# Mean squares from the transposed input: the opening of a hybrid encoder step on one core

## The chip, the core and the metric

The kernel runs on one core of a Trainium2 chip. Five engines work side by side, each through its own instructions in order: TensorE (PE in the profile; its weight loads are PEld), VectorE (DVE), ScalarE (ACT), GpSimd (POOL) and SyncE (SP), which here only issues DMA transfers. The metric is the device time of one execution in microseconds (us), lower is better. The matrix products run in a reduced single-precision form (float32r): each operand is split into a high and a low part, and three products (high by high, high by low, low by high) stand for one.

## The reference, cut to what matters

One step of a one-layer encoder. Prompt frames (1024) and sample frames (8 streams of 16, so 128) are normalised, projected by one large matrix into eight groups of 1024 columns, go through two kinds of attention, are gated, and are projected back. What the change touches is the normalisation ahead of the first projection:

```python
def rms_norm(x, g):
    xf = x.astype(jnp.float32)
    y = xf * lax.rsqrt(jnp.mean(xf * xf, axis=-1, keepdims=True) + EPS)
    return (y * g.astype(jnp.float32)).astype(x.dtype)
...
    h = rms_norm(xp, norm_pre[l])
    q_sb, k_sb, v_sb, gate_sb, q_r, k_r, v_r, gate_r = project(h, w_in[l], pos_p)
```

The width of a frame (D_MODEL) is 2048, so each frame has one mean square over 2048 elements.

## The kernel before, in words

The frames are taken in two groups. Group 0 holds prompt tiles 0 to 3 and the sample tile, 640 frames, in two pieces of 256 and 384 frames (`X_PIECES`); group 1 holds the other four prompt tiles, 512 frames. For projection the input must lie transposed: 128 of the 2048 features on the partitions, frames along the free axis. Sixteen blocks (`KT`) of 128 features make the whole. The host hands over the transposed input as `x_cols`; the input by rows (`x_rows`) is there as well.

The opening (the `p0` pools, lines 489 to 563) does this for group 0, one piece after the other:

- `load_x` (L503) brings row tiles of 128 frames by 2048 (1 MB each, two buffers of tag `xt`), and `mean_square` (L514) squares each in one ScalarE instruction that also sums along the row. The first piece has two row tiles, the second three.
- `inv_rms` (L173 to L179) makes the inverse root of the mean: VectorE scales and adds, ScalarE takes the root, VectorE takes the reciprocal and corrects it in four steps. The operand has one column a row tile.
- `spread` turns that column into a row, the same on all partitions: VectorE puts it on a diagonal (`dg`, L522), TensorE multiplies by a matrix of ones in full single precision (L524, two records a product in the trace), and ScalarE copies the result (`rb`, L525).
- `load_cols` (L510) brings the transposed input of the piece in four chunks of four blocks (`xc`, four buffers). `normal` multiplies a block by the gain and by `rb`: odd blocks by ScalarE (gain, L530) and GpSimd (`rb`, L531), even ones by VectorE in one instruction (L533). `split` (L164, L165) makes the high part by ScalarE and the low part by VectorE.
- `products` (L378) multiplies the blocks by the panels of two weight columns, 4 and 5 (the retention queries and keys of head 0): twelve instructions a panel and quarter, so 96 a piece. Panels are loaded in four parts (`wr`, 256 KB each, five buffers shared by all weight loads; L367 and L548) and split like the input. Both panels' parts are kept, because both pieces need them.

Behind the opening follow the rotary step of both results (`rope`, L468 to L472), the retention values (`ret_values`, rows of weights as moving operand, L434) and the gate. Beside these a job, `stage_rest`, prepares group 1 in the same manner: it loads four row tiles, squares them, spreads the result, scales sixteen blocks and stores them to `s_h` by ScalarE's queue (L587). A job is a generator; every product calls `tick`, which lets a due job take one step, and the number that a job yields is the count of ticks until its next step. Group 1 itself is loaded from `s_h` much later (L248, buffers `mr`).

The order of the instructions on each engine isn't written out: a planner goes through the program by order of writing and by its own costs, and puts an instruction ahead of others written earlier when these aren't ready by its reckoning. `pin` keeps an instruction, in that planning alone, behind the last product written so far. Each engine then works strictly in the planned order. The accumulators lie in four PSUM banks (`acc0`, `acc1`, two each), which both panels' results hold until the rotary step has read them; `pb` has four banks of its own.

Of the kernel before, what the change touches and what calls it, by code (L numbers as in the profile page):

```python
# [11 lines left out]
F32 = mybir.dt.float32  # L12
F32R = mybir.dt.float32r
AF = mybir.ActivationFunctionType
ALU = mybir.AluOpType
# [73 lines left out]
def tile_hybrid_step(  # L89
# [358 lines left out]
    with ExitStack() as s1:  # L448
# [42 lines left out]
        with tc.tile_pool(name="p0", bufs=2) as p0, tc.tile_pool(name="p0s", bufs=1) as p0s, tc.tile_pool(  # L491
# [9 lines left out]
            def load_x(t):  # L501
                xt = p0.tile([P, D], F32, name="xt", tag="xt", bufs=2)
                nc.sync.dma_start(xt, x_rows(t))  # L503
                return xt

            def load_cols(piece, k, m):
                o, n = X_PIECES[piece]
                xc = p0.tile([P, m, n], F32, name=f"xc{piece}", tag="xc", bufs=4)
# [4 lines left out]
            def mean_square(xt, ssq, i):  # L513
                nc.scalar.activation(xt, xt, AF.Square, accum_out=ssq[:, i : i + 1])  # L514

            def spread(ssq, n, hold=None):
                rstd = inv_rms(p0, ssq[:, :n], D, f"p0{n}")
# [10 lines left out]
            def normal(dst, xc, k, rb, pool):  # L528
                if pool:
                    nc.scalar.activation(xc, xc, AF.Copy, scale=pre[:, k : k + 1])  # L530
                    nc.gpsimd.tensor_tensor(dst, xc, rb, ALU.mult)  # L531
                else:
                    nc.vector.scalar_tensor_tensor(dst, xc, pre[:, k : k + 1], rb, ALU.mult, ALU.mult)  # L533

            tiles = g0["tiles"]
            accs = [acc_banks(g0), acc_banks(g0)]
            at = 0
            weights4 = []
            for piece, n in enumerate((2, 3)):
                o, m = X_PIECES[piece]  # L540
                ssq = p0s.tile([P, n], F32, name=f"ssq{n}")
                xts = [load_x(t) for t in tiles[at : at + n]]
                xcs = [load_cols(piece, w * WQ, WQ) for w in range(KT // WQ)]
                if piece == 0:
                    weights4 = [list(load_w(col(4, 0))), []]
                    for w in range(KT // WQ):
                        wr = wp.tile([P, WQ, P], F32, name="wr", tag="wr", bufs=5)
                        nc.sync.dma_start(wr, w_cols[COLS.index(5), 0, :, w * WQ : (w + 1) * WQ, :])  # L548
                        wh, wl = (p0s.tile([P, WQ, P], F32R, name=f"w{s}5{w}") for s in "hl")
                        split(wh, wl, wr)  # L550
                        weights4[1].append((w, wh, wl))
                for i, xt in enumerate(xts):
                    mean_square(xt, ssq, i)
# [992 lines left out]
```

## Time and profile before

| | |
|---|---|
| median of 3 runs | 2297.87 us (2295.14 to 2300.01) |
| the profiled execution | 2302.97 us, span 2301.2 us |
| TensorE busy | 2242.1 us, 97% of the span |
| VectorE, ScalarE, GpSimd busy | 54%, 40%, 16% |
| TensorE's first weight product | 17.61 us after the span's start |
| moved by DMA | 470.99 MB, mean 205 GB/s |

The profiled execution is 5.1 us above the median, and 1.8 us of it lie around the span. Rows of the trace in order of time give the start, the duration (of several merged instructions together), the engine, the line, the operation, the tiles written and read, shapes and count; in brackets stands how long the engine was idle before it and what it waited for. Rows of groups give busy time, mean duration in ns, idle time before, and its causes. Rows of stages give from and to, the length, busy time and count for each engine (TensorE, weight load, VectorE, ScalarE, GpSimd), the clock granted to TensorE as a share of full speed, the DMA engines' share and GB/s; where the rows are those of one line alone, only the engines that this line uses stand in them. A queue that issues DMA transfers has a q behind its engine (SPq).

### The profile page before, as it was taken

The numbers are of one execution on the slowest core, as the hardware profiler recorded it, in microseconds if no ns is written. First come the engines' busy times: TensorE is split into PE (matmuls) and PEld (weight loads), VectorE is DVE, ScalarE is ACT, GpSimd is POOL, SyncE is SP. The second block draws the span as 40 slices with busy tenths as digits, with TensorE's granted clock in tenths as the row PEclk, the third lists the DMA queues.
The fourth block names the chain that finished last, engine by engine and source line by source line (L and its number), as shares of the span: only waits on it lengthen the run. The fifth ranks groups of instructions, "written<-read, shape, count | busy, mean of one in ns | idle before, by whom it ended". The sixth has DMA issues, their size and how long they took to land.

```text
span 2301.2 us, 38949 instructions
## 1 busy us (share of the span) xinstructions
PE 2242.1 (97%) x14306; PEld 2021.9 (88%) x14306; DVE 1236.9 (54%) x2534; ACT 919.4 (40%) x1960; POOL 357.5 (16%) x593
## 2 busy tenths in 40 slices
PE   5999999999999999999999999999999999999998
PEld 4999999999999999999887989898888987788886
DVE  6534444354534435356556565656565566556577
ACT  6423333333333333334433433343343444535363
POOL 2012030120203021121102111120212212000020
PEclk9999999999999999999999999999999999999999
DMA  7856657565566658568778788778787767766596
GB/s 282 280 186 195 190 151 223 175 191 195 148 194 199 197 159 229 169 185 266 198 214 224 218 213 236 211 231 223 220 220 224 211 167 186 238 215 185 142 224 175
DMA packets 441552, 470.99 MB, mean 205 GB/s; under 512 B 182416, under 2 KB 302224, under 8 KB 439696
## 3 DMA queue, kind: packets, MB, share of 16 engines
q1 hardware_dynamic: 318112, 304.09, 46.3%
q0 software_dynamic: 28720, 78.41, 12.1%
q10 hardware_dynamic: 94528, 86.00, 11.8%
q8 instruction: 112, 1.84, 0.3%
q14 instruction: 80, 0.66, 0.1%
HBM read 363.51 MB, written 114.29 MB: 208 GB/s over the span
## 4 chain that ended last, share of the span: by engine, by line
PE 87%; DMA 6%; DVE 3%; issue 2%; ACT 2%; POOL 0%; SPq 0%; DVEq 0%; ACTq 0%; POOLq 0%
PE acc L378 46%; PE accn L434 16%; PE a L1179 5%; PE a L1180 5%; PE a L1176 5%; PE pa L762 2%; PE z L732 2%; PE zc L801 1%; PE pd L865 1%; DMA s_be<-be 1%; DMA ro<-s_rk 1%; DMA be<-s_be 1%; PE pa L910 1%; DMA s_rk<-rk 1%; DMA xt<-x_prompt 1%
## 5 line engine op out<-in xcount | busy, mean ns | idle before, releaser
L378 PE MATMUL acc<-mh,wh 128*128 128x256 f32 (+2 forms) x2304 | 668.0, 341 | 7.2 <-ACT wh L164 4.4
L378 PE MATMUL acc<-ml,wh 128*128 128x256 f32 (+2 forms) x2304 | 664.3, 340 | 1.2 <-DVE ml L165 1.1
L378 PE MATMUL acc<-mh,wl 128*128 128x256 f32 (+2 forms) x2304 | 661.0, 339 | 1.3 <-DVE wl L165 1.3
L165 DVE TENSOR_TENSOR wl<-wr,wh 128x512 fp32r<-128x512 f32 x504 | 346.0, 689 | 468.0 <-ACT wh L164 450.2
L164 ACT ACTIVATE wh<-wr 128x512 fp32r<-128x512 f32 x504 | 316.9, 631 | 651.1 <-PE acc L378 331.6
L378 PEld LDWEIGHTS acc<-mh,wh 128*128 128x128 f32 x2304 | 421.8, 189 | 40.0 <-ACT wh L164 4.9
L378 PEld LDWEIGHTS acc<-ml,wh 128*128 128x128 f32 x2304 | 423.3, 189 | 34.2 <-issue 3.3
L378 PEld LDWEIGHTS acc<-mh,wl 128*128 128x128 f32 x2304 | 426.0, 189 | 29.8 <-DVE wl L165 2.0
L434 PE MATMUL accn<-whn,mh 128*128 128x256 f32 x1152 | 328.8, 285 | 1.3 <-DVE rq L471 0.9
L434 PE MATMUL accn<-wln,mh 128*128 128x256 f32 x1152 | 325.9, 283 | 0.0
L434 PE MATMUL accn<-whn,ml 128*128 128x256 f32 x1152 | 325.5, 283 | 0.0
L434 PEld LDWEIGHTS accn<-whn,mh 128*128 128x128 f32 x1152 | 220.8, 192 | 4.5 <-ACT whn L164 1.7
L434 PEld LDWEIGHTS accn<-wln,mh 128*128 128x128 f32 x1152 | 220.8, 192 | 0.8
L434 PEld LDWEIGHTS accn<-whn,ml 128*128 128x128 f32 x1152 | 220.5, 192 | 0.0
L165 DVE TENSOR_TENSOR wln<-wrn,whn 128x512 fp32r<-128x512 f32 x128 | 87.7, 687 | 140.6 <-ACT whn L164 139.2
L164 ACT ACTIVATE whn<-wrn 128x512 fp32r<-128x512 f32 x128 | 80.6, 633 | 190.0 <-PE accn L434 92.9
L625 POOL DMA_DIRECT2D be<-s_be x128 | 94.1, 741 | 155.6 <-DMA s_be<-be 132.8
L661 DVE TENSOR_TENSOR_SCAN kp<-kp 128x1152 f32<-128x1152 f32 (+4 forms) x40 | 82.7, 2067 | 53.5 <-POOL kp L650 36.9
L650 POOL TENSOR_SCALAR_AFFINE_SELECT kb<-kb 128x128 f32<-128x128 f32 x64 | 30.5, 484 | 439.1 <-ACT kb L644 436.8
L788 POOL DMA_DIRECT2D kcT<-cache_k x64 | 34.6, 545 | 404.4 <-PE pd L865 268.9
L1179 PE MATMUL a<-wl,mh 128*128 128x512 f32 x240 | 93.6, 390 | 0.2 <-DVE wl L165 0.2
L1180 PE MATMUL a<-wh,ml 128*128 128x512 f32 x240 | 93.6, 390 | 0.0
(272 smaller groups left out, 2950.5 us busy)
## 6 DMA issues: line engine op xcount, KB each, us to landing
wr<-w_cols SPq DMA_DIRECT2D x384, 256.0 KB, 4.5
wrn<-w_rows SPq DMA_DIRECT2D x128, 256.0 KB, 3.8
kcT<-cache_k POOLq DMA_DIRECT2D x64, 512.0 KB, 8.3
vc<-cache_v SPq DMA_DIRECT2D x64, 512.0 KB, 5.8
wr<-s_b SPq DMA_DIRECT2D x80, 256.0 KB, 4.0
br<-w_out SPq DMA_DIRECT2D x64, 256.0 KB, 5.1
s_b<-br ACTq DMA_DIRECT2D x32, 512.0 KB, 5.4
wr<-w_out SPq DMA_DIRECT2D x48, 256.0 KB, 4.0
```

What stands on the lines that cost most here:

```text
L164: nc.scalar.activation(hi, src, AF.Copy),
L165: nc.vector.tensor_tensor(lo, src, hi.bitcast(F32), ALU.subtract),
L378: last = nc.tensor.matmul(a[:, :m], lhs[:, j, :], rhs[w][:, j, o : o + m], start=(w == 0 and j == 0 and n == 0), stop=(w == KT // WQ - 1 a ...
L434: anchor[0] = nc.tensor.matmul(a, lhs[q][:, jj, ts], rhs[:, j, :], start=(w == 0 and j == 0 and n == 0 and t % 2 == 0), stop=(w == KT // 2 ...
L625: q.dma_start(raw[32 * i : 32 * i + 32, :].rearrange("p (k a) -> p k a", a=32), s[:, :, 32 * i : 32 * i + 32].rearrange("k (j b) a -> b (k ...
L661: nc.vector.tensor_tensor_scan(rev, rev, rev, 1.0, ALU.mult, ALU.bypass)
L732: nc.tensor.matmul(z[:, :c], q2[a][:, i * P : (i + 1) * P], k2[b][:, s : s + c], start=(m == 0), stop=(m == 2),)
L762: nc.tensor.matmul(po[:, :P], at[:, j, :], vn[:, j, :], start=(j == 0), stop=(j == t))
L788: ready.append((kc, nc.gpsimd.dma_start(kc, cache_k[h, m // 4, m % 4])))
L1176: ins = nc.tensor.matmul(a, hi[k][:, ts], wh, start=first, stop=False)
L1179: nc.tensor.matmul(a, hi[k][:, ts], wl, start=False, stop=False)
L1180: anchor[0] = nc.tensor.matmul(a, lo[k][:, ts], wh, start=False, stop=last)
```

## The change

The mean squares of group 0 no longer come from row tiles. ScalarE squares the transposed blocks, and TensorE multiplies each by the matrix of ones and adds the sixteen results up in a PSUM bank; so the sums stand on all partitions at once, and `spread` is not called for group 0. `inv_rms` now works on the whole 128x256 or 128x384 operand. For the second piece GpSimd adds the squares of two neighbouring blocks first, so that eight products do. These squares are written in between the first piece's products: two chunks' worth after the second quarter, two after the third, pinned behind the products. The scaling (`normal`) is VectorE's alone. The order of the loads is written anew: transposed chunks of the first piece, then the parts of both panels, with second-piece chunks between; first-piece and second-piece chunks have four buffers each. The high parts of the second panel lie in the `mr` buffers. In `stage_rest` the row tiles are loaded and squared in halves of 1024 columns, with longer yields (10 for 6 after a load), and two partial sums are added.

```diff
             def load_x(t):
-                xt = p0.tile([P, D], F32, name="xt", tag="xt", bufs=2)
-                nc.sync.dma_start(xt, x_rows(t))
-                return xt
+                halves = []
+                for c in range(2):
+                    xt = p0.tile([P, HALF], F32, name="xt", tag="xc0", bufs=4)
+                    nc.sync.dma_start(xt, x_rows(t)[:, c * HALF : (c + 1) * HALF])
+                    halves.append(xt)
+                return halves
...
             def mean_square(xt, ssq, i):
-                nc.scalar.activation(xt, xt, AF.Square, accum_out=ssq[:, i : i + 1])
+                for c, half in enumerate(xt):
+                    pin(nc.scalar.activation(half, half, AF.Square, accum_out=ssq[:, c, i : i + 1]))
...
-            def normal(dst, xc, k, rb, pool):
-                if pool:
-                    nc.scalar.activation(xc, xc, AF.Copy, scale=pre[:, k : k + 1])
-                    nc.gpsimd.tensor_tensor(dst, xc, rb, ALU.mult)
-                else:
-                    nc.vector.scalar_tensor_tensor(dst, xc, pre[:, k : k + 1], rb, ALU.mult, ALU.mult)
+            def normal(dst, xc, k, rb):
+                nc.vector.scalar_tensor_tensor(dst, xc, pre[:, k : k + 1], rb, ALU.mult, ALU.mult)
...
+            totals = [p0p.tile([P, 512], F32, name=f"tot{i}", tag="pb")[:, :n] for i, (_, n) in enumerate(X_PIECES[:2])]
+            xcs = [[load_cols(0, w * WQ, WQ) for w in range(KT // WQ)], []]
+
+            def squares(piece, w):
+                sq = None
+                for j in range(WQ):
+                    k = w * WQ + j
+                    one = p0.tile([P, X_PIECES[piece][1]], F32, name=f"sq{piece}", tag=f"sq{j % 2}")
+                    pin(nc.scalar.activation(one, xcs[piece][w][:, j, :], AF.Square))
+                    if piece and j % 2 == 0:
+                        sq = one
+                        continue
+                    if piece:
+                        nc.gpsimd.tensor_tensor(one, one, sq, ALU.add)
+                    nc.tensor.matmul(totals[piece], ones, one, start=(k <= piece), stop=(k == KT - 1))
+
+            for w in range(KT // WQ):
+                squares(0, w)
...
+            first_panel = load_w(col(4, 0))
+            both_panels = [], []
+            for w in range(KT // WQ):
+                both_panels[0].append(next(first_panel))
+                both_panels[1].append(load_second(w))
+                if w:
+                    xcs[1].append(load_cols(1, (w - 1) * WQ, WQ))
+            xcs[1].append(load_cols(1, KT - WQ, WQ))
+            for piece, (o, m) in enumerate(X_PIECES[:2]):
+                rb = inv_rms(p0s, totals[piece], D, f"p0{piece}")
                 for w in range(KT // WQ):
                     for j in range(WQ):
                         k = w * WQ + j
-                        xn = p0.tile([P, m], F32, name=f"xn{piece}", tag="xn", bufs=3)
-                        normal(xn, xcs[w][:, j, :], k, rb, k % 2)
+                        xn = p0.tile([P, m], F32, name=f"xn{piece}", tag="xn", bufs=2)
+                        normal(xn, xcs[piece][w][:, j, :], k, rb)
                         split(mov[0][w][:, j, o : o + m], mov[1][w][:, j, o : o + m], xn)
-                    for acc, ws in zip(accs, weights4):
+                    for acc, ws in zip(accs, both_panels):
                         last = products(mov, acc[piece : piece + 1], g0["pieces"][piece : piece + 1], *ws[w])
-                at += n
+                    if piece == 0:
+                        for c in ((), (0, 1), (2, 3), ())[w]:
+                            squares(1, c)
```

More of the change, by code (lines that the diff above doesn't have):

```diff
@@ L539, in tile_hybrid_step @@
[L539 to L553, printed above, removed]
-                rb = spread(ssq, n)
+            def normal(dst, xc, k, rb):
+                nc.vector.scalar_tensor_tensor(dst, xc, pre[:, k : k + 1], rb, ALU.mult, ALU.mult)
```

23 lines of the change are left out of this document (14 added, 9 removed).

## The prediction

> **What bounds the kernel now.** I read the page first, then TensorE in order of time over the first 100 us, then the other engines there, and last the groups by form for prices.
>
> ```profile
> PE 2242.1 (97%) x14306; PEld 2021.9 (88%) x14306; DVE 1236.9 (54%) x2534; ACT 919.4 (40%) x1960; POOL 357.5 (16%) x593
> ```
>
> TensorE is busy for 97% of the span, so only time in which it stands still or runs at half clock can be won. The change touches nothing but the opening and the staging behind it. There TensorE goes like this (start, duration):
>
> ```profile
> 17.61 0.58 PE L378 MATMUL acc<-mh,wh 128*128 128x256 f32 x1 [3.56 <-ACT wh L164]
> ...
> 22.87 0.41 PE L378 MATMUL acc<-mh,wh 128*128 128x256 f32 x1
> 23.08 0.41 PE L378 MATMUL acc<-ml,wh 128*128 128x256 f32 x1
> ...
> 23.87 0.28 PE L378 MATMUL acc<-mh,wh 128*128 128x256 f32 x1
> 23.98 0.28 PE L378 MATMUL acc<-ml,wh 128*128 128x256 f32 x1
> ...
> 34.43 0.28 PE L378 MATMUL acc<-mh,wl 128*128 128x256 f32 x1
> 40.09 1.97 PE L524 MATMUL pb<-dg,ones 128*128 128x128 f32 x6 [5.38 <-DVE dg L522]
> 44.06 1.01 PE L378 MATMUL acc<-mh,wh 128*128 128x384 f32 x2 [2.00 <-ACT mh L164]
> ...
> 45.53 0.52 PE L378 MATMUL acc<-mh,wl 128*128 128x384 f32 x1
> 45.85 0.52 PE L378 MATMUL acc<-mh,wh 128*128 128x384 f32 x1
> ...
> 64.86 0.29 PE L434 MATMUL accn<-whn,mh 128*128 128x256 f32 x1
> ...
> 67.55 0.36 PE L434 MATMUL accn<-whn,mh 128*128 128x256 f32 x1 [0.85 <-DVE rq L471]
> ...
> 71.72 0.35 PE L434 MATMUL accn<-whn,mh 128*128 128x256 f32 x1 [0.46 <-DVE rk L471]
> ```
>
> The first piece's 96 products run from 17.61 to 34.7. A gap of 9.4 us follows, broken by three small products. The second piece's 96 run from 44.06 to 64.86. Spacing tells the clock: 0.21 us for 256 columns until 23.08, 0.11 to 0.12 from 23.87 on; 0.32 us for 384 columns at 45.53. The granted clock fell in the gap and came back 7.2 us after TensorE took up work at 40.09:
>
> ```profile
> 37.00:38.00 1.00, 0.00 (x0) 0.00 (x0) 0.00 (x0) 1.00 (x2) 0.00 (x0) 0.56 0.98 393
> ...
> 46.00:47.00 1.00, 1.00 (x5) 1.00 (x4) 1.00 (x2) 0.63 (x2) 0.45 (x2) 0.50 1.20 225
> 47.00:48.00 1.00, 1.00 (x7) 1.00 (x6) 1.00 (x2) 0.84 (x2) 1.00 (x1) 0.82 0.64 197
> ...
> 55.00:60.00 5.00, 4.89 (x29) 4.58 (x28) 1.00 0.01 2
> ```
>
> The last row counts the products of L378 alone: 5.0 / 29 = 0.172 us each at full clock. Why the gaps are there stands on the other engines:
>
> ```profile
> 1.26 0.90 SPq L503 DMA_DIRECT2D xt<-x_prompt  x2
> ...
> 6.37 1.91 ACT L514 ACTIVATE xt<-xt 128x2048 f32<-128x2048 f32 x1 [4.06 <-DMA xt<-x_prompt]
> ...
> 8.89 1.91 ACT L514 ACTIVATE xt<-xt 128x2048 f32<-128x2048 f32 x1 [0.52 <-DMA xt<-x_prompt]
> ...
> 10.93 0.17 DVE L173 TENSOR_SCALAR p02v<-ssq 128x2 f32<-128x2 f32 x1 [9.28 <-ACT xt L514]
> ...
> 12.21 0.16 DVE L179 TENSOR_TENSOR p02r<-p02r,p02u 128x2 f32<-128x2 f32 x1
> ...
> 14.09 0.38 ACT L525 ACTIVATE rb<-pb 128x256 f32<-128x256 f32 x1 [0.70 <-PE pb L524]
> ...
> 28.59 0.33 SPq L503 DMA_DIRECT2D xt<-x_sample  x1
> ...
> 36.14 1.91 ACT L514 ACTIVATE xt<-xt 128x2048 f32<-128x2048 f32 x1 [3.09 <-DMA xt<-x_sample]
> ```
>
> Each row tile of 1 MB takes 2.52 us of transfer (6.37 to 8.89). The last one is issued at 28.59, when a buffer comes free, and lands at 36.1. Squares, root, spreading and rb follow; so the second piece waits for rows that exist only for their squares.
>
> **The change, part by part.** Times are those of the profiled execution; differences go onto the median of 2297.87.
>
> *Loads.* Five row tiles leave SP's queue, 12.6 us of transfer. The first xc chunk (half a tile's bytes) takes the first row tile's place and lands at 6.37 less half of 2.52, 5.1; the fourth at 8.9. The panels follow, with second-piece chunks between them. SP still waits for free wr buffers (five), now with second-piece chunks queued behind it.
>
> *First sums.* ScalarE squares a 128x256 block in 0.41 (cast row below), so TensorE starts at 5.5, into two of the pb banks. Nothing in the trace shows a sum of 256 columns; nearest is L524, in the same full-precision form with 128:
>
> ```profile
> 84.67 0.71 PE L524 MATMUL pb<-dg,ones 128*128 128x128 f32 x4
> 85.14 0.36 PE L434 MATMUL accn<-whn,ml 128*128 128x256 f32 x1
> ...
> L164 ACT ACTIVATE mh<-xn 128x256 fp32r<-128x256 f32 x16 | 5.8, 405 | 2.2 <-POOL xn L531 2.2
> L164 ACT ACTIVATE mh<-xn 128x384 fp32r<-128x384 f32 x16 | 7.9, 520 | 7.1 <-POOL xn L531 6.5 <-DVE xn L533 0.5
> L295 DVE TENSOR_TENSOR br<-br 128x256 f32<-128x256 f32 x192 | 80.3, 418 | 7.5 <-DMA br<-s_y 5.6
> L470 DVE TENSOR_TENSOR sw<-sw,sinT 128x384 f32<-128x384 f32 x16 | 8.9, 558 | 15.4 <-ACT sw L469 15.4
> L175 DVE RECIPROCAL or<-or 128x5 f32<-128x5 f32 x8 | 1.5, 189 | 8.1 <-ACT or L174 8.1
> L175 DVE RECIPROCAL or<-or 128x1 f32<-128x1 f32 x8 | 1.3, 158 | 1.0 <-ACT or L174 1.0
> L179 DVE TENSOR_TENSOR or<-or,ou 128x5 f32<-128x5 f32 x8 | 1.3, 166 | 0.3
> L179 DVE TENSOR_TENSOR or<-or,ou 128x1 f32<-128x1 f32 x8 | 1.3, 158 | 0.2
> ```
>
> The four records are two products; they took 0.47 at full clock (84.67 to 85.14), so one of 256 columns takes 0.24 (if width were free) to 0.47 (if time goes with columns). Columns rule elsewhere (0.11 at 256, 0.172 at 384), so I take 0.43, and 0.86 at half clock. In the opening the half clock lasted from 17.61 to past 23.08; I take 5.5 us: six and a half sums in that, nine and a half in 4.1. Totals stand at 5.5 + 5.5 + 4.1 + 0.2 = 15.3. Ends: 14.2 if the clock comes after the 3.3 us that passed between 44.06, when work became continuous, and the 0.82 slice; 19.5 if never. The Trainium skill, "TensorE: Matmul & The Clock Gate", Part 1, says that about 3.4 us of sustained work in a free-running window release the clock; by it the totals would stand at 14.3, one microsecond earlier, and this trace's 5.5 and 7.2 us (both with pauses) are longer.
>
> *Root chain, now 128x256.* Seven steps took 10.93 to 12.37 = 1.44 us at two columns. Widening adds 0.25 to each of four tensor steps (0.418 against 0.16), 0.21 to the root (0.405 against 0.19), 0.2 to a scalar step: 1.4. The reciprocal is unknown: +0.26 if it goes as TENSOR_TENSOR, +1.8 if its narrow slope (31 ns over four elements, 7.8 each) holds to 256. TENSOR_TENSOR's own narrow slope (8 ns, 2.0 each) is twice its wide one ((558 - 418) / 128 = 1.09), so I halve: +1.0. Spreading (dg, pb, rb) goes. The factors stand at 15.3 + 0.1 + 1.44 + 1.4 + 1.0 = 19.2, against 14.47 (14.09 + 0.38) before: 4.8 later. Ends 18.5 and 20.0.
>
> *First piece's products.* Block 0 needs a scaling, a cast and the semaphores: first product at 20.3 (17.61 before). VectorE now scales all sixteen blocks:
>
> ```profile
> 22.52 0.47 DVE L533 SCALAR_TENSOR_TENSOR xn<-xc,pre,rb 128x256 f32<-128x256 f32 x1
> ...
> 30.32 1.09 DVE L165 TENSOR_TENSOR ml<-xn,mh 128x256 fp32r<-128x256 f32 x3
> ...
> 47.20 1.38 DVE L165 TENSOR_TENSOR ml<-xn,mh 128x384 fp32r<-128x384 f32 x1
> ...
> L531 POOL TENSOR_TENSOR xn<-xc,rb 128x384 f32<-128x384 f32 x8 | 10.3, 1282 | 17.8 <-ACT rb L525 10.7 <-DVE ml L165 6.0 <-POOL xn L531 1.1
> ```
>
> Back to back that is 0.41 + 0.36 = 0.77 a block, 12.3 in all. Beside a GpSimd operation VectorE's 0.56 became 1.38, so each of the eight pair additions holds it up by 0.8: 6.6. Sum 18.9, until 38.1. TensorE needs 96 x 0.117 = 11.2, 2.5 more for 26 products at half clock (5.5 / 0.21, each 0.095 longer; it stood still from 15.3 to 20.3), and eight sums of 384 columns at 0.64 = 5.1: until 39.1. So the first piece ends at 39.1, not 34.7. ScalarE's sixteen squares of 0.52 stand in one queue with the casts; 14 us of its work fit beside 19. The panels' splits go into VectorE's wait before 19.2 and cost nothing while that wait lasts.
>
> *Second factors.* The additions of GpSimd (10.3 us) can start when the first half of the products is issued, about 26.6, so totals stand at 37.8. The chain at 384 columns: 1.44 + 4 x 0.39 + 0.33 + 0.25 + reciprocal 1.5 (0.4 to 2.9) = 5.1, and 0.3 of scaling beside it. Factors at 43.2, first product 1.2 later at 44.4, against 44.06: the gap that the rows made is filled by a later first piece and a wider chain.
>
> *Second piece.* TensorE has stood still for 5.3 us and starts at half clock: 17 products at 0.32, 79 at 0.172, together 19.0 (20.8 before, when GpSimd's scaling held VectorE up). VectorE needs sixteen times 1.05. End 63.4 against 64.86: 1.4 earlier.
>
> *Behind it.* The stalls at 67.55 and 71.72, 1.3 us, are acc banks whose rope copies stood behind 1.91 us squares on ScalarE. Halved and pinned squares take about 0.8 of that. The additional read-outs, VectorE's one addition, the longer yields and the later s_h stores cost nothing while ScalarE, VectorE and SP have slack there, and the mr buffers lent to the second panel are free by then; SP's mr loads wait for those stores, and if they came much later, panel loads behind them would be late. No GpSimd transfer lies in this stretch to be moved past.
>
> Sum: -1.4 - 0.8 = -2.2, from 2297.87 to 2295.7, inside the 0.2% (4.6 us) that a measurement of this kernel can tell from no change.
>
> **The rivals.**
>
> *The gaps close (faster).* Full clock fell by 37.4 (the 0.56 row), 2.7 us after 34.7. If the reciprocal costs like TENSOR_TENSOR, 0.7 and 1.1 us go, and if the second totals are ready some 2 us before the products end, the wait for the second factors is short enough to keep the clock: 2.5 more, and the overlap itself 1. Together 5.3 below the forecast: 2290.4. For it: GpSimd's additions are off the path; against it: its start hangs on ScalarE's queue.
>
> *Reciprocal at its narrow slope (no change).* 0.8 and 1.4 us more: 2297.9. The rows at one and five elements speak for it; no wide one is shown. The Trainium skill, "VectorE: DVE Perf Modes", "First, the fixed hardware budget", says that the reciprocal is an iterative divide with a repeat count of 8; read as eight cycles an element at its 0.96 GHz, an estimate, that is 2.1 and 3.2 us, and the time would be the same 2297.9. No run here shows it yet.
>
> *ScalarE's queue (slower).* Squares wait for sum buffers that GpSimd and TensorE give back, and casts behind them wait along. If the eight squares of a quarter pair stand ahead of its casts, the additions (5.1 us for four) run before the quarter's scaling and not beside it: per quarter 5.1 + 0.9 + 3.1 + 1.0 = 10.1 for 6.3, twice +3.8, and a TensorE without products: +7.6, 2303.3. It decides when six or more squares stand ahead. For it: ScalarE stood idle 6.5 us for GpSimd's results with casts behind (384 cast row above). Against it: a planner that sees the wait puts casts between.
>
> **How the numbers follow.** Forecast 0.32, slow reciprocal 0.12, gaps closed 0.32, ScalarE's queue 0.24. The first two are within 0.2%: 0.44; faster 0.32, slower 0.24. Term ends from the forecast: clock -1.0 to +4.2, reciprocal -1.8 to +2.2, hold-up by GpSimd 0 to -3 (half of the 6.6 where VectorE waits anyway), stalls -0.5 to +0.8. The forecast's own range is 2292 to 2299; over the cases it reaches from 2287 (gaps closed, and the clock early) to 2305 (the queue, and the clock late).
>
> **What would show it.** First sums at 5.5, their last near 15; a 256-wide reciprocal near 1.2 us; first product near 20, last of the first piece near 39; TensorE idle 5 us ahead of 44; last product of the second piece near 63; no waits of 0.8 for rope afterwards. The prediction is wrong if sums stay at 0.86, if casts wait more than 2 us behind squares, if the panels' splits on VectorE delay the first chain, or if a panel load stands behind a stalled SP queue.

## The result

The changed kernel takes 2315.98 us (median of 4 runs, 2311.55 to 2318.23), the kernel before 2297.36 beside it: a ratio of 1.0078, 95% interval 1.006 to 1.0097, so 18.6 us slower. A second set on another chip gave 1.0073 (1.0058 to 1.0088). The prediction was 2295.7, no change, with a range of 2287 to 2305: the sign of the change was missed.

The profiled execution of the changed kernel has a span of 2314.0 us (2301.2 before). Its engine totals:

```profile
PE 2258.5 (98%) x14344; PEld 2035.3 (88%) x14344; DVE 1245.4 (54%) x2546; ACT 918.4 (40%) x1972; POOL 348.6 (15%) x585
```

TensorE in order of time (start, duration), the changed kernel:

```profile
5.50 9.88 PE L551 MATMUL tot<-sq,ones 128*128 128x256 f32 x32 [5.50 <-ACT sq L545]
25.06 0.80 PE L378 MATMUL acc<-mh,wh 128*128 128x256 f32 x2 [9.68 <-ACT mh L164]
...
46.98 0.28 PE L378 MATMUL acc<-mh,wl 128*128 128x256 f32 x1
...
54.42 0.69 PE L378 MATMUL acc<-mh,wh 128*128 128x384 f32 x1 [7.16 <-ACT mh L164]
...
74.30 0.34 PE L378 MATMUL acc<-mh,wl 128*128 128x384 f32 x1
...
76.46 0.36 PE L434 MATMUL accn<-whn,mh 128*128 128x256 f32 x1 [0.29 <-DVE rq L471]
...
149.24 0.79 PE L931 MATMUL pa<-rv,sc 128*128 128x128 f32 x2 [6.14 <-DVE sc L915]
```

Two separate losses show. The opening (up to the second piece's last product) ends at 74.6 instead of 65. And at 149 there is a wait of 6.1 us that the kernel before doesn't have, far behind the code that changed. Stages of the changed kernel (from and to, length, busy time of TensorE, weight load, VectorE, ScalarE, GpSimd, granted clock, DMA share, GB/s):

```profile
40.00:60.00 20.00, 12.24 (x55) 9.79 (x54) 14.98 (x26) 9.10 (x20) 4.12 (x4) 0.83 0.14 43
...
140.00:160.00 20.00, 13.86 (x87) 13.67 (x86) 5.79 (x15) 3.98 (x12) 0.00 (x0) 0.83 0.51 154
```

In 40 to 60 the DMA engines move 43 GB/s (194 before, where two of group 1's row tiles are issued at 45.39 and 46.34; in the changed kernel such a load goes out last at 41.18), and no compute engine waits for a transfer there: the 7.16 us ahead of 54.42 are a wait for ScalarE's cast, which waits for VectorE's chain. In 140 to 160 TensorE stands still for 6.1 us (busy for all 20 us before). Until about 154.5 it then runs at half pace, two products in 0.53 us instead of 0.30, so the stall costs more than its length.

### The profile page after: what moved, and what is told of

Its sections match the earlier page's. It is cut to its first block, busy times and chain, and to the rows that moved or that the text cites. A ratio compares the mean times of both kernels' runs of the same rounds, so it can differ in the third digit from the quotient of the medians.

```text
span 2314.0 us, 39042 instructions
## 1 busy us (share of the span) xinstructions
PE 2258.5 (98%) x14344; PEld 2035.3 (88%) x14344; DVE 1245.4 (54%) x2546; ACT 918.4 (40%) x1972; POOL 348.6 (15%) x585
## 4 chain that ended last, share of the span: by engine, by line
PE 86%; DMA 6%; DVE 3%; issue 2%; ACT 2%; SPq 1%; POOL 1%; ACTq 0%; DVEq 0%; POOLq 0%
PE acc L378 46%; PE accn L434 16%; PE a L1200 5%; PE a L1201 5%; PE a L1197 5%; PE pa L783 2%; PE z L753 2%; PE zc L822 1%; PE pd L886 1%; DMA s_be<-be 1%; DMA wr<-w_cols 1%; DMA ro<-s_rk 1%; DMA be<-s_be 1%; PE pa L931 1%; PE pS L946 1%
## 5 line engine op out<-in xcount | busy, mean ns | idle before, releaser
L1197 PE MATMUL a<-wh,mh 128*128 128x512 f32 x240 | 93.4, 390 | 0.8 <-ACT wh L164 0.8
```

The source lines that it names most:

```text
L1197: ins = nc.tensor.matmul(a, hi[k][:, ts], wh, start=first, stop=False)
```

## The second loss: a collision of transfers

The staging is the job `stage_rest` that prepares group 1. Early runs changed its yields alone.

**e1**: the changed kernel with yields of 6.

```diff
-                    yield 10
+                    yield 6
```

> The changed kernel with the waits of stage_rest back at 6 ticks after a load (10 in the changed kernel). Theory A, two separate losses: the opening (first product of the retention values at 74.5 us, 64.9 before) and a later stall of 6.1 us at the first retention block of head 0, which comes because group 1's staging ends 17 us later (last s_h store issued at 124.4, 107.3 before), so that the cache loads of GpSimd's queue start at 130.8 (114.5 before) and run beside the turned keys' loads. By A the last store is issued near 115, the cache loads start before 122, the stall falls below 2 us, and the time is about 2308 (7 to 8 below the changed kernel's 2316). Rival B, the stall follows from the opening's lateness alone: stores move by less than 3 us, the stall stays near 6 us, time within 2 us of 2316.

Measured 2312.98, 1.0062 (1.0043 to 1.008). The wait shrank to 3.7 us only, and the last store came at 121.3: 3 us earlier, where theory A asked for 9. This run lies between A and B and decides little.

**e2**: the kernel before with yields of 10 (the same edit the other way).

> The kernel before with only the waits of stage_rest raised from 6 to 10 ticks after a load. Theory A: the last s_h store moves from 107.3 to about 116, the cache loads from 114.5 to about 122, and a stall at the first retention block comes up: 2300 to 2305 (before: 2297). Rival B, the waits matter only behind a late opening: within 2 us of 2297.

Measured 2303.68, 1.0023 (1.0014 to 1.0033), 6.6 us above the kernel before on its chip: longer yields alone cost time, and a wait of 4.5 us appears at the same products.

**e7**: the changed kernel with yields of 2.

> The changed kernel, with the staging's yields after loads at 2 instead of 10. Theory A (the end of the staging is a loss of its own: memory freed late, GpSimd's cache loads beside the transposing transfers): the last store to s_h comes at 102 to 107 (124.4 with 10, 121.3 with 6), the cache loads start near 110 (130.8), the 6.1 us stall at the sample scores is under 1.5, the first z product comes near 157 (163.2), and the time is 6 to 7 us lower, near 2309.5. Rival B (the stall comes from the later opening itself, whatever the staging does): the stall stays above 4 us and the time above 2313.

Measured 2309.52, 1.005 (1.0034 to 1.0066). The wait is gone, and the first z product (L753, the next attention scores) came at 157.6, as theory A has it, though the last store came at 116.9, 10 us later than it asked. So the time of the stores alone is not what decides. What decides is which of two kinds of transfer goes out first, and by how much. The rows, the changed kernel first: VectorE's first write into the memory that the opening gives back, GpSimd's loads of cached keys, SP's transposing loads, and the instruction that needs these, with its wait.

```profile
130.21 0.06 DVE L660 MEMSET kp<- 128x1 f32 x1 [3.46 <-DMA s_h<-xc]
...
130.82 3.39 POOL L809 DMA_DIRECT2D kcT<-cache_k  x6 [85.24 <-DMA wrn<-w_rows]
...
131.60 4.75 SPq L646 DMA_DIRECT2D ro<-s_rk  x4
...
146.77 0.84 DVE L1032 STREAM_TRANSPOSE rkn<-ro 128x640 f32<-128x640 f32 x1 [9.13 <-DMA ro<-s_rk]
```

The kernel before:

```profile
114.47 3.40 POOL L788 DMA_DIRECT2D kcT<-cache_k  x6 [54.41 <-DMA wr<-w_cols]
...
120.48 6.06 SPq L625 DMA_DIRECT2D ro<-s_rk  x4
...
131.50 0.84 DVE L1011 STREAM_TRANSPOSE rkn<-ro 128x640 f32<-128x640 f32 x1 [0.86 <-DMA ro<-s_rk]
```

The cache loads (six of 512 KB, issued within 3.4 us) go out when the opening's memory is free, and the last staged chunk must be stored for that: without the hold below, they start 5.4 to 8.6 us behind the issue of the last store in every run. VectorE's `kp` names that store as what it waited for; for GpSimd's first load the profile names a weight load. The transposing loads stand in SP's queue behind weight loads, which wait for buffers that VectorE's splits give back. In the changed kernel VectorE itself stands for the last store first (the row of `kp`), and SP's queue with it, so that both kinds of transfer follow the same store. Before, the cache loads had a lead of 6.0 us over the transposing ones; now 0.8, and `ro<-s_rk` takes 13.4 us to land (median of its four) instead of 9.8. VectorE's transposition waits 9.1 us, the scores behind it make TensorE wait 6.1. Over the runs the lead sorts the waits without exception: with 5.1 us or more (e7 5.1, e9 5.9, the kernel before 6.0, e14 6.1, e13 6.4, e12b 10.1, e16 12.7) there is no such wait; with 2.8 (e2) and 3.0 (e1) it is 4.5 and 3.7 us; with 0.8 or less (the changed kernel, e3, e4, e5b, e6, e10, e14c, e17) it is 5.2 to 7.2 us.

**e14c**: is it the staging or the late opening? The kernel before with VectorE's scaling (e9, below) and the changed staging, but with rows for the mean squares.

```diff
-                        normal(xn, xcs[w][:, j, :], k, rb, k % 2)
+                        normal(xn, xcs[w][:, j, :], k, rb, False)
...
-                    xt = load_x(t)
-                    yield 6
-                    mean_square(xt, ssq, i)
+                    xt = p0.tile([P, D], F32, name="xt", tag="xt", bufs=2)
+                    for c in range(2):
+                        cs = slice(c * D // 2, (c + 1) * D // 2)
+                        nc.sync.dma_start(xt[:, cs], x_rows(t)[:, cs])
+                    yield 10
+                    for c in range(2):
+                        cs = slice(c * D // 2, (c + 1) * D // 2)
+                        pin(nc.scalar.activation(xt[:, cs], xt[:, cs], AF.Square, accum_out=ssqs[:, c, i : i + 1]))
...
-                    yield 6
+                    yield 10
```

> The kernel before with scaling by VectorE alone and with the changed staging (halves squared one by one and pinned, yields 10): of the change everything but the squares of the transposed blocks and the order of the opening's loads. Theory A (the staging costs when its last stores come too late, about 107 or later): the opening ends some 8 us earlier than in the kernel before, so with yields 10 the last store comes at 102 to 106 instead of 97.7, no wait at the sample scores, 2293 to 2296, within 2 us of the kernel with scaling by VectorE alone. Then the whole loss belongs to the squares of the transposed blocks, and the staging costs only where the opening is late. Rival (the longer yields cost their 6.5 us in any opening): 2298 to 2301.

Measured 2300.84, 1.0014 (1.0004 to 1.0024): the rival. The opening is early, and yet the last store comes at 108.2 (theory A: 102 to 106), the lead is 0.55 us and the wait 5.2:

```profile
115.30 3.37 POOL L795 DMA_DIRECT2D kcT<-cache_k  x6 [113.92 <-DMA wrn<-w_rows]
...
115.85 6.71 SPq L632 DMA_DIRECT2D ro<-s_rk  x4
...
PE pa L917 <- DVE sc L901: 5.2, 1, 5.2
```

**e18 and e19**: the changed kernel, and e14c, with the cache loads held behind the landing of `ro<-s_rk`, while the staging stays as late as it is.

```diff
+        turned_rk = []
...
             def load_k(m):
                 kc = ip.tile([P, 2, 512], F32, name="kcT", tag="kv", bufs=V_BUFS)
+                if h == 0 and m == 0:
+                    nc.gpsimd.tensor_copy(kc[:, 0, :2], turned_rk[0][:, :2])
                 ready.append((kc, nc.gpsimd.dma_start(kc, cache_k[h, m // 4, m % 4])))
...
+            while h == 0 and not turned_rk:
+                yield 3
             for m in range(KC_AHEAD):
                 load_k(m)
...
             turn_in(s, raw, nc.sync)
+            turned_rk.append(raw)
```

> The changed kernel, with GpSimd's first six loads of cached keys held behind the landing of head 0's transposing transfers ro<-s_rk (a copy of two columns into the first buffer makes them wait); nothing else differs. Theory A2 (the second loss is a collision: 3 MB of cache loads issued within 3 us ahead of those small transfers): ro<-s_rk lands after 5 to 7 us instead of 13, the wait of 6 to 7 us at the score products goes to under 1, the first z product comes near 156, and the time is 5 to 7 us below the changed kernel's, 2309 to 2311, though the staging ends as late as before. Rival (the late staging itself costs, or the cache loads are then late for their own products): the wait stays above 3 us or moves to the cache products, time 2313 or more.

> The same hold in the kernel with scaling by VectorE alone and the changed staging (2300.8 without the hold). Theory A2: its 5.2 us wait goes, 2293.5 to 2296; the changed staging then costs nothing that can be measured beside scaling by VectorE alone. Rival: 2299 or more.

Measured 2307.78, 1.004 (1.0025 to 1.0055), and 2292.19, 0.9968 (0.9958 to 0.9977). Rows of e18:

```profile
130.16 2.18 SPq L646 DMA_DIRECT2D ro<-s_rk  x4
...
135.72 0.18 POOL L812 COPY kcT<-ro 128x2 f32<-128x2 f32 x1 [91.54 <-DMA wrn<-w_rows]
136.30 3.38 POOL L813 DMA_DIRECT2D kcT<-cache_k  x6 [0.39 <-issue]
```

The four loads go out nearly as late as before (130.16, 131.60) and now land after 3.6 us (median; 3.4 in e19), the wait is gone from TensorE's list in both, no product waits for the cache loads, and the first z product comes at 153.5 (163.2; the opening ended 0.9 us earlier in this execution). The collision is shown to be the cause: it takes 7.5 us of the changed kernel's loss (2315.31, measured again as e17, less 2307.78) and 8.6 us of e14c's. Where on their way the two kinds of transfer hold each other up, no run shows. By the intervals of the ratios each of the two differences is uncertain by some 3 to 5 us. The hold was not run in the kernel before or in e14; that e19 comes to e14's ratio (0.9968 and 0.997) suggests that it has little to gain there.

> The changed kernel as it is, once more beside these: 1.0065 to 0.0015 either side of 1.0078 times the kernel before, 20 to 25 us above the kernel with scaling by VectorE alone.

Measured 2315.31, 1.0073 (1.0058 to 1.0088).

## The first loss: the opening

Rows of VectorE in the changed kernel, the first chain:

```profile
15.44 1.52 DVE L165 TENSOR_TENSOR wl<-wr,wh 128x512 fp32r<-128x512 f32 x2 [0.94 <-ACT wh L164]
16.88 0.42 DVE L173 TENSOR_SCALAR p00v<-tot 128x256 f32<-128x256 f32 x1
17.78 1.75 DVE L175 RECIPROCAL p00r<-p00r 128x256 f32<-128x256 f32 x1 [0.48 <-ACT p00r L174]
19.45 1.22 DVE L165 TENSOR_TENSOR wl<-wr,wh 128x512 fp32r<-128x512 f32 x2
...
21.83 0.42 DVE L179 TENSOR_TENSOR p00r<-p00r,p00u 128x256 f32<-128x256 f32 x1
```

The totals are there at 15.4, but the chain's first step (`p00v`) starts at 16.88, behind two panel splits, and two more lie inside the chain: the factors are ready at 22.25. The cast that the first product needs then stands on ScalarE behind casts of panels that are late:

```profile
22.49 0.63 ACT L164 ACTIVATE wh<-wr 128x512 fp32r<-128x512 f32 x1 [2.83 <-DMA wr<-w_cols]
24.07 0.63 ACT L164 ACTIVATE wh<-wr 128x512 fp32r<-128x512 f32 x1 [0.96 <-DMA wr<-w_cols]
24.61 0.40 ACT L164 ACTIVATE mh<-xn 128x256 fp32r<-128x256 f32 x1
```

They are late because SP's queue stood from 6.32 to 12.71 for a free wr buffer (five are given out by then), and the first panel's cast on ScalarE came only at 11.35, behind squares that went at the pace of TensorE's sums.

**e3**: sums as single products in float32r, which removes that pace. **e4**: two more buffers for the second panel's parts, which removes SP's wait. The first part shown is e3's, the second e4's.

```diff
-                    one = p0.tile([P, X_PIECES[piece][1]], F32, name=f"sq{piece}", tag=f"sq{j % 2}")
+                    one = p0.tile([P, X_PIECES[piece][1]], F32R, name=f"sq{piece}", tag=f"sq{j % 2}")
...
-                wr = wp.tile([P, WQ, P], F32, name="wr", tag="wr", bufs=5)
+                if w < 2:
+                    wr = p0.tile([P, WQ, P], F32, name="wr5", tag="wr5", bufs=2)
+                else:
+                    wr = wp.tile([P, WQ, P], F32, name="wr", tag="wr", bufs=5)
```

> The changed kernel with the sums of squares made in the reduced form (float32r) and not in full single precision; the squares lose low bits. Theory C, the sums' pace sets the start: TensorE's full-precision sums take 9.9 us, give square buffers back at 0.86 us each, ScalarE's panel casts stand behind the squares, and SP's queue stands until a panel buffer is free (12.7 us). By C the first totals stand near 11 (15.4 in the changed kernel), the sixth panel part is issued before 10, the first product comes near 20 (25.1), and the time falls by 4 to 6 us to 2310 to 2312. Rival D, the panel transfers and VectorE's wide chain set it anyway: first product after 23, time within 2 us of 2316.

> The changed kernel with two buffers more for the second panel's raw parts, so that SP's queue does not stand from 6.3 to 12.7 us behind a full set of panel buffers. Theory C: the last panel part lands near 18 and not near 24, no cast of the first block stands behind a wait for it, the first product comes near 22.5 (25.1), 2 to 3 us less time: about 2313. Rival D, squares hold the casts in any case: first product within 1 us of 25, time within 1 us of 2316.

Measured 2312.61, 1.0064 (1.0049 to 1.0079), and 2313.65, 1.0065 (1.0049 to 1.008). The first product comes at 21.74 and 23.34, the second piece ends at 71.0 and 74.0. In the five executions whose opening is the changed kernel's own (the changed kernel, e1, e7, e17, e18) these come at 23.82 to 25.06 and at 73.8 to 74.6. So e3's effect is clear, 2 to 3 us at the first product and as much at the end; e4's is 0.5 to 1.7 us at the first product and not to be seen at the end. In e3 the totals stood at 11.3, 4 us early, and the chain still took until 20.2, because panel splits that waited for their DMA stood inside it. Against the changed kernel neither time is separated by its interval.

**e6**: the wide reciprocals taken of one column.

```diff
-        nc.vector.reciprocal(r, r)
+        one = r[:, :1] if name in ("p00", "p01") else r
+        nc.vector.reciprocal(one, one)
```

> The changed kernel with both wide reciprocals taken of one column alone, the other columns left out (their factors are then not inverse roots). It prices them. If both lie on the path: 1.75 - 0.17 and 2.54 - 0.17 us, so 4.0 us lower, 2312. If the first one is covered by the panels that ScalarE's casts wait for (the first product stood behind a cast at 24.61): the first product stays at 24.5 to 25.1, only the second counts, 2.4 us lower, 2313.6.

Measured 2310.67, 1.005 (1.0034 to 1.0065). First product at 22.35, second piece's first at 49.77 (54.42, and 53.03 to 54.42 in the five executions). Both reciprocals lie on the path, 1.75 us at 256 columns and 2.54 at 384; without them the second piece begins 3.3 to 4.7 us earlier.

**The first piece and the second totals.** ScalarE and GpSimd during the first piece, the changed kernel:

```profile
32.02 1.75 ACT L545 ACTIVATE sq<-xc 128x384 f32<-128x384 f32 x4
34.27 0.53 ACT L545 ACTIVATE sq<-xc 128x384 f32<-128x384 f32 x1 [0.50 <-POOL sq L550]
34.70 0.40 ACT L164 ACTIVATE mh<-xn 128x256 fp32r<-128x256 f32 x1
...
35.14 0.43 DVE L165 TENSOR_TENSOR ml<-xn,mh 128x256 fp32r<-128x256 f32 x1 [1.77 <-ACT mh L164]
```

VectorE waits for casts behind squares: 1.77, 1.08, 1.76 and 1.49 us. This looked like the cause. **e5b** takes the squares away from ScalarE and leaves GpSimd's and TensorE's part:

```diff
-                    pin(nc.scalar.activation(one, xcs[piece][w][:, j, :], AF.Square))
-                    if piece and j % 2 == 0:
-                        sq = one
-                        continue
-                    if piece:
-                        nc.gpsimd.tensor_tensor(one, one, sq, ALU.add)
+                    if piece and j % 2 == 0:
+                        continue
+                    if piece:
+                        pin(nc.gpsimd.tensor_tensor(one, xcs[piece][w][:, j, :], xcs[piece][w][:, j, :], ALU.mult))
+                    else:
+                        pin(nc.scalar.activation(one, xcs[piece][w][:, j, :], AF.Square))
```

> The changed kernel without ScalarE's sixteen squares of the second piece: GpSimd multiplies each odd block by itself instead of adding two squares, so its eight operations and TensorE's eight sums of 384 columns stay, at the same places; the even blocks' squares are left out of the second totals. Theory E (the first piece was long because casts mh stood behind the squares in ScalarE's queue): VectorE's waits of 1.1 to 1.8 us for mh go, the first piece's last product comes at 40 to 41 instead of 47.0, the second piece's first at 47 to 48.5 instead of 54.4, and the time is 6 to 7.5 us below the changed kernel's, near 2309. Rival F (the eight GpSimd operations hold VectorE up, and TensorE's sums stand between the products): these stay, the first piece ends after 45, and the time is at most 2 us lower, 2314 or more.

Measured 2316.3, 1.0089 (1.0063 to 1.0115): theory E fell. The waits of VectorE went (0.5 us are left of 6.1), but the first piece ended at 46.5 (47.3) and the second began at 51.76. Counted from its own first product, at 25.50, the first piece took 21.0 us instead of 22.2. The stretch 34 to 47 says why; TensorE's whole work in it, then that of the sums alone, in the changed kernel:

```profile
34.00:47.00 13.00, 12.02 (x65) 8.70 (x63) 6.68 (x13) 8.05 (x20) 7.30 (x8) 1.00 0.52 175
...
34.00:47.00 13.00, 6.99 (x16) 2.39 (x16) 1.00 0.52 175
```

TensorE is shown busy for 12.0 of 13.0 us, 7.0 of them with the eight sums of 384 columns (two records each); in e5b it is 11.56. These records, 0.87 us a sum, overlap with those of the products behind them. By the starts a sum holds the next product up by 0.69 to 0.83 us at full clock, 0.75 on average, where 0.64 was forecast. With the squares gone, TensorE and GpSimd, which waits 2.62 us for TensorE to give a buffer back, end last.

**e10**: the same squares one quarter earlier.

```diff
-                        for c in ((), (0, 1), (2, 3), ())[w]:
+                        for c in ((0, 1), (2, 3), (), ())[w]:
```

> The changed kernel with the second piece's squares written one quarter earlier: two chunks behind the first quarter's products, two behind the second's. Theory I (the second totals are set by the place that is written, behind the third quarter's products, with sums and additions sharing two buffers): totals at 39.5 to 41 instead of 46.5, the second chain lies beside the last quarter, the second piece's first product comes at 48 to 50 instead of 54.4, time 4.5 to 6.5 us below the changed kernel's, 2309.5 to 2311.5. Rival F (the squares, additions and sums lengthen the first piece wherever they stand, and the chain then delays its last scalings): the second piece's first product at 52 or later, time 2314 or more.

Measured 2315.34, 1.0062 (1.0048 to 1.0076). The second chain starts at 43.03 (46.58), but now scalings lie inside it, VectorE's four waits are nearly as long as before (5.5 us, 6.1), and the second piece begins at 51.74. It ends at 73.5, where the five executions end at 73.8 to 74.6. Theory I is right about the totals and wrong about the gain. **e12b** takes the second piece's squares out of the first piece altogether, and changes the sums, the loads and the yields with it. Of the edit, the part on the squares:

```diff
-            xcs = [[load_cols(0, w * WQ, WQ) for w in range(KT // WQ)], []]
+            xcs = [[load_cols(i, w * WQ, WQ) for w in range(KT // WQ)] for i in range(2)]
...
-            for w in range(KT // WQ):
-                squares(0, w)
+            for piece in range(2):
+                for w in range(KT // WQ):
+                    squares(piece, w)
```

> The changed kernel rearranged: the second piece's transposed chunks are loaded straight behind the first piece's, all 32 squares are taken ahead of the first product, the sums are single products with float32r operands (the squares lose low bits), GpSimd adds nothing, panels are loaded behind, and the staging yields 2 after a load. By theories A, C and E together nothing of the three losses is left: first chain without panel splits inside, first product at 18 to 20, no gap between the pieces (the second chain of 5 us lies beside the first piece's products), last product of the second piece at 56 to 59 (64.7 in the kernel before, 74.3 in the changed one), last store to s_h before 107, time 2287 to 2291. Rival: the second piece's squares and the panels' late arrival hold the first product past 23 and VectorE, with both chains and all splits, is the bound until past 64; time 2296 or more.

Measured 2295.62, 0.9993 (0.9983 to 1.0003): between theory and rival. First product at 21.28, a gap of 0.8 us between the pieces (7.2), last product at 61.93, last store at 101.5, no wait at the scores. 20 us of the changed kernel's time are won back by the order, the float32r sums and the short yields together; their shares were not run one by one. It is not below 2291 because the 384-wide reciprocal (2.55 us at 29.95) now stops the first piece's low parts, TensorE waits 2.18 us and runs at half clock from 32.83 to 38.8.

## The gain inside the change

**e9** and, beside e13, **e14**: the kernel before with scaling by VectorE alone.

```diff
-                        normal(xn, xcs[w][:, j, :], k, rb, k % 2)
+                        normal(xn, xcs[w][:, j, :], k, rb, False)
```

> The kernel before, with VectorE alone scaling the blocks; row tiles, spreading, loads and staging stay. Theory G (this part of the change is a small gain): the first piece's VectorE work becomes 16 x 0.85 + 8 x 0.69 = 19.1 us beside 17.1 that the piece took, so it ends up to 2 us later, which the wait for the third row tile hides; the second piece, 20.8 us before, takes 17.5 to 19; time 2294 to 2297.5. Rival H (VectorE becomes the bound of both pieces): second piece 20 us or more and the first piece's end past 38; time 2299 or more.

> The kernel before with scaling by VectorE alone, once more, beside the kernel with the third buffer: 2293 to 2296, 0.1% to 0.3% below the kernel before.

Measured 2294.17, 0.998 (0.997 to 0.999), and 2292.93, 0.997 (0.9959 to 0.9982): faster than the kernel before, by 4.6 to 6.5 us, as theory G has it. TensorE in e14:

```profile
16.65 0.58 PE L378 MATMUL acc<-mh,wh 128*128 128x256 f32 x1 [2.75 <-ACT wh L164]
...
37.41 0.63 PE L378 MATMUL acc<-mh,wh 128*128 128x384 f32 x2 [1.79 <-ACT mh L164]
...
57.21 0.34 PE L378 MATMUL acc<-mh,wl 128*128 128x384 f32 x1
```

The second piece begins at 37.4 (e14) and 39.9 (e9), at 44.06 before. Its row tiles are loaded earlier (in e14 the first at 11.41 instead of 19.64, the last at 24.66 instead of 28.59) and squared earlier. The edit touches only the scaling, but the planner made another order for it: the first of these row tiles now stands in SP's queue ahead of a panel part that in the kernel before waited for a buffer until about 19. How much of the gain is the scaling itself and how much this order was not run.

**e13**: a third row buffer on top, so that the last row tile is not held up. **e16**: yields of 2 on top of e9. The edit shown is e13's.

```diff
-                xt = p0.tile([P, D], F32, name="xt", tag="xt", bufs=2)
+                xt = p0.tile([P, D], F32, name="xt", tag="xt", bufs=3)
...
-                        wh, wl = (p0s.tile([P, WQ, P], F32R, name=f"w{s}5{w}") for s in "hl")
+                        wh = wp.tile([P, WQ, P], F32R, name="wh5", tag="mr", bufs=MR)
+                        wl = p0s.tile([P, WQ, P], F32R, name=f"wl5{w}")
```

> The kernel before with scaling by VectorE alone and a third buffer for row tiles (the second panel's high parts lie in the mr buffers to make room). By the reading that the third row tile's wait for a buffer makes the gap between the pieces: with scaling by VectorE alone its load was issued at 24.9 and the second piece began at 39.9, 3.9 us after the first had ended; with a third buffer it is issued near 20.6, squared by 31, and the second piece begins 1 us behind the first's end, 36 to 37: 3 us below the kernel with scaling by VectorE alone, near 2291. Rival: the earlier megabyte delays the panels that the first piece needs, the first piece ends that much later, and the time is the same as without the buffer.

> The kernel before with scaling by VectorE alone and yields of 2 after the staging's loads. If the staging matters only through the wait at the scores, which is not there with scaling by VectorE alone, the earlier staging gives nothing: last store near 90, time within 2 us of 2293. Rival: the row tiles and chunks, loaded closer together, come ahead of the weights, TensorE waits for those in 60 to 100, and the time is 2 to 4 us higher.

Measured 2291.86, 0.9975 (0.9962 to 0.9987), and 2294.7, 0.9985 (0.9975 to 0.9995). The third buffer brings the tile's load to 20.41, but the second piece begins at 38.0, no earlier than e14's: the time is near the forecast and no different from e14's, as the rival has it. From the first piece's end to the second's first product 3.3 us pass in e9, e14 and e13 alike, and in e14 the last square (29.84) waits for no transfer. So what is left between the pieces is the chain behind that square (root, spreading, scaling, cast) and not the row tile. Earlier staging (e16) gives nothing once the lead is long enough. Of all versions e19, e14 and e13 are the fastest and can't be told apart; e9 and e16 lie below the kernel before as well.

## Why the prediction was wrong, step by step

In the runs of e14c, e17, e18 and e19 the kernel before took the same time (2298.96 and 2298.88). All four scale by VectorE alone, and they split the rest of the change:

| | squares from row tiles | squares from transposed x |
|---|---|---|
| changed staging | 2300.84 | 2315.31 |
| and cache loads held back | 2292.19 | 2307.78 |

The transposed squares, with the order of loads that goes with them, cost 14.5 and 15.6 us, the collision that the changed staging makes 8.6 and 7.5, and scaling by VectorE gains 4.6 to 6.5 (e9, e14).

- *Loads.* "SP still waits for free wr buffers" was said and priced at nothing; it made the panels late. Without that wait (e4) the first product comes 0.5 to 1.7 us earlier.
- *First sums*: forecast 15.3, measured 15.38. Half the pace until about 11.3, 5.8 us after the start, as taken from the trace. The Trainium skill, "TensorE: Matmul & The Clock Gate", Part 1, has the clock released after some 3.4 us of sustained work; this trace has 5.8. The forecast was right, in part by luck: the half pace lasts 6.3 us behind 25.06 and 4.4 behind 54.42. But the pace also held ScalarE, and so the first panel's cast, until 11.35; that was not seen.
- *Root chain*: 19.2 forecast, 22.25 measured. The reciprocal was 1.75 us, 0.6 above what was taken (+1.0) and near the upper end (+1.8). The larger part, 2.5 us, failed in the sentence "the panels' splits go into VectorE's wait before 19.2 and cost nothing while that wait lasts": two stood ahead of the chain when the totals were there, and two inside it.
- *First piece's products*: first product 20.3 forecast, 25.06 measured; end 39.1 forecast, 47.3 measured. Nearly 5 of the 8 us came in with the start. The other 3.4 can be read off the starts of TensorE's rows: eight sums at 0.75 and not 0.64, 0.9 us; half pace for 6.3 us and not 5.5, 0.6; three waits of sums for GpSimd's additions, 1.5 (1.0 of it shown as idle); the rest in small pieces. On VectorE the hold-up by GpSimd, forecast at 6.6 us, was 1.3 (low parts of 1.49 and 1.03 us instead of 0.82 and 0.42). In its place VectorE waited 6.1 us for casts behind squares, in four waits that each stay below the 2 us named as a sign: the rival *ScalarE's queue* is in sight, but not as the only cause (e5b).
- *Second factors*: totals 37.8 forecast, about 46.5 measured; the gap of 5.3 us became 7.2, of which the 384-wide reciprocal is 2.54 (1.66 forecast).
- *Second piece*: 19.0 forecast, 20.2 measured, at half clock for 4.4 us (5.4 forecast).
- *Behind it*: the rope stalls went almost entirely (0.29 left of 1.3). But the sentence that the later s_h stores "cost nothing while ScalarE, VectorE and SP have slack there" is the step that failed outright. I looked at SP's reads of the stores and at GpSimd's transfers ahead of them ("no GpSimd transfer lies in this stretch to be moved past"), and stopped the stretch too early: the stores also free the memory behind which GpSimd's cache loads wait, and at 130.82 those met the transposing loads. That is 7.5 us.
- *Scaling by VectorE alone*, counted inside the sums above and never by itself, was the one gain that a run shows.

The sign failed because costs of one serial opening (splits, SP's wait, squares, later stores) were each put into another engine's wait, and several of these waits were no longer there.

## What to carry to other kernels

A chain widened from a column to a whole tile pays for its width at each step (here 0.42 us instead of 0.16, the reciprocal 1.75 instead of 0.17), and work of other chains that lies in the same engine's order gets inside it; look at what the planner can put between its steps before calling it covered. When a staging job ends later, follow the memory that it frees: a prefetch that starts by itself when a buffer comes free moves along with it, and may meet small transfers that had a free path; holding such a prefetch behind them made no product wait here and gained 7.5 and 8.6 us. When a change is a bundle, run its parts alone: here the part that seemed incidental was the only one that gained.

## What the runs showed that I had not expected

- Four transposing loads of 80 KB land after 3.2 to 3.8 us when the 3 MB of cache loads are held behind them (e18, e19). With these issued 12.7 us ahead the median is 3.1 us (e16), 6.0 us ahead 9.8 (the kernel before), and 0.8 us ahead 13.4 (the changed kernel).
- The reciprocal costs 6.6 to 6.8 ns an element of the free axis (1753 and 2542 ns for 256 and 384), four times a tensor by tensor product (0.42 for 256):

```profile
L175 DVE RECIPROCAL p00r<-p00r x1: 1753/1753/1753, 17.8 to 17.8; 128x256 f32<-128x256 f32 x1
L175 DVE RECIPROCAL p01r<-p01r x1: 2542/2542/2542, 48.3 to 48.3; 128x384 f32<-128x384 f32 x1
```

  The Trainium skill, "VectorE: DVE Perf Modes", "First, the fixed hardware budget", gives a repeat count of 8; read as eight cycles at 0.96 GHz, an estimate, that is 2.1 and 3.2 us, so the measured slope is lower.
- The granted clock of TensorE is shown as 1.00 in the first 15 us of the changed kernel, although its sums went at 0.86 us each until about 11.3 and at about 0.43 behind that: in the opening the spacing tells the clock, not the record.
